# A re-ordered opening in an eight-core decoder layer

## The chip, the cores and the metric

The kernel runs on all 8 NeuronCores of one Trainium2 chip as one program, each core with an eighth of the tokens. The metric is device time in microseconds (us) of the slowest core. A core has TensorE (PE in the profile), VectorE (DVE), ScalarE (ACT), GpSimd (POOL) and SyncE (SP); cores 0 to 3 and 4 to 7 lie on two dies.

In some executions the cores of one die run at a lower granted clock, and the time is some per cent longer whatever the kernel. Such runs are called slow here, and are never set against fast ones. In two of the three batches of experiments (e1 to e4, e5 to e8, e9 to e12) one die was slow in many or all runs. There I compare the *undisturbed die*: of every run in which all four clocks of a die were above 0.99, the mean span of its four cores, averaged over the runs, with its standard error. Even there the mean clock lies between 0.996 and 1.000, and 0.001 of it is 1.2 us. So I also give some means *at equal clock*: each core's span times the granted clock on record for it, an estimate of the span had the clock never fallen. A difference that is gone at equal clock is one of the clock and not of the waits.

## The reference, cut to what matters

```python
h = rms_norm(x, g)
z = h @ w_in                    # columns: q 1024 | k 256 | v 256 | GLU value 1024 | GLU gate 1024
a = attn_prompt(q, k, v)        # window 128, q and k normed and rotated; 32 sample tokens use a cache
c = silu(layer_norm(causal_dwconv(u_val * sigmoid(u_gate))))   # width 31
x = x + concat([a, c]) @ w_out
x = x + relu(rms_norm(x) @ w_up) ** 2 @ w_down                 # hidden 8192
```

x is float32, 8192 prompt tokens and 32 sample tokens of 2048 features. A core multiplies 1032 to 1160 columns (tokens) at a time.

## The kernel before

The program records every operation of every engine in program order. A list scheduler then simulates time with fixed costs and emits, for each engine, the order in which its simulation could start the operations. Each engine executes that order strictly. One constant of this simulation is the DMA rate:

```python
    LAT = {"pe": 200, "act": 110, "dve": 110, "pool": 150}
    DMA_NS = 2000
    DMA_RATE = 290.0
    # ... cut ...
                if u[0].is_dma:
                    st = max(end, dma_free)
                    dma_free = st + u[0].nbytes / self.DMA_RATE
                    fin = dma_free + self.DMA_NS
```

The opening loads x in 16 chunks of 128 features, scales each to bf16 (`HT`), and multiplies it at once with the key and value weights. The query weights come after x:

```python
    for kc in range(16):
        xs_ = XST[kc % 8]
        xd.append(dma("sp", xs_(), R(xt_d[kc]), ..., after=[xd[kc - 6]] if kc >= 6 else []))
        dma("pool", WKV(kc), R(wkv_d[kc]), ..., after=[xd[max(kc - 4, 0)]] if kc >= 2 else [])
        ts("dve", HT(kc), xs_(), G1(kc), ALU.mult)
        # ... sums of squares cut ...
        for i in range(2):
            for h in range(2):
                mm(kps[i](h), WKV(kc, (128 * h, 128 * h + 128)), HT(kc, KPC[i]), kc == 0, kc == 15)
        for ti in range(8):
            v_mm(ti, vps[ti], kc, ...)
```

The output projection makes 16 blocks, each of 24 matmuls into three neighbouring PSUM banks, which VectorE then adds to x. Even blocks use banks 0 to 2; odd blocks 3 to 5 at first, later 4 to 6. Between them stand the last convolution and the statistics of the LayerNorm, which use banks 6 and 7:

```python
    def wo_half(dc, half, src, b0):
        accb = Buf("ps", psum[:, b0:b0 + 3, :], b0 * 2048, (3, 512), 4)
        # ... 24 matmuls into accb ...
        tt("dve", x3(), accb((0, 3), (0, PW)), x3(), ALU.add)

    def ln_stats():
        for pi, (a, b) in enumerate(PM):
            pm, pv = ps_f32(6, 1, (PW,)), ps_f32(7, 1, (PW,))      # banks 6 and 7
            # ... cut ...

    def wo_first(i):
        wo_half(DCO[i], 0, AT, 0 if i % 2 == 0 else 3 if i < 7 else 4)
        # ... cut ...

    for i in range(3):
        wo_first(i)
    conv_job(7, 0)
    # ... cut ...
    for i in range(3, 5):
        wo_first(i)
    ln_stats()
    for i in range(5, 16):
        wo_first(i)
```

## Time and profile before

| | before |
|---|---|
| median of three runs | 1233.95 us |
| spans of the cores in the profiled run | 1224.8 to 1233.1 us |
| TensorE busy, slowest core | 1195.2 us, 97% |
| idle of TensorE, mean of 8 cores: to 60 us / 60 to 150 / 150 to 320 / 320 to the MLP | 20.7 / 1.2 / 0.0 / 7.9 us |
| MLP: start, length, waits of TensorE (means) | 437.6, 791.0, 2.4 us |

The idle times are the length of a stretch less the busy time of TensorE in it, from the table by stretches, on every core; the MLP is taken to start with the run of matmuls that begins with the form 128x258 float32.

The table by stretches (the first column after the stretch is its length, then TensorE's busy time and, in brackets, its matmuls; the last columns are granted clock, DMA share, GB/s):

```profile
356.00:359.00 3.00, 3.00 (x12) 1.55 (x11) 3.00 (x3) 1.25 (x1) 0.00 (x0) 0.50 0.80 141
363.00:366.00 3.00, 3.00 (x23) 2.05 (x21) 3.00 (x3) 2.29 (x2) 0.00 (x0) 1.00 0.98 154
```

For about 3 us after the waits TensorE ran at half its clock: 12 matmuls in 3 us instead of 23. The cost is 12.30 - 72 x 0.149 = 1.6 us that no wait shows. Cores 0, 3, 4 and 5 have it (0.83 for the mean clock from 350 to 360 us). Cores 1, 2, 6 and 7 have the same waits of 1.55 and 2.06 us, keep a clock of 1.00, and do the same 72 matmuls in 10.62 us. What differs is how the waits fall into windows of 3.41 us. In the trace the stretches at half clock here last 3.41 us, and each follows 3.41 us in which TensorE did little.

### The profile page before, as it was taken

The numbers are of one execution on the slowest core, as the hardware profiler recorded it, in microseconds if no ns is written. First come the engines' busy times: TensorE is split into PE (matmuls) and PEld (weight loads), VectorE is DVE, ScalarE is ACT, GpSimd is POOL, SyncE is SP. The second block draws the span as 40 slices with busy tenths as digits, with TensorE's granted clock in tenths as the row PEclk, the third lists the DMA queues.
The fourth block names the chain that finished last, engine by engine and source line by source line (L and its number), as shares of the span: only waits on it lengthen the run. The fifth ranks groups of instructions, "written<-read, shape, count | busy, mean of one in ns | idle before, by whom it ended". The sixth has DMA issues, their size and how long they took to land.

```text
span 1233.1 us, 26343 instructions; the slowest of 8 cores (1224.8 to 1233.1 us)
## 1 busy us (share of the span) xinstructions
PE 1195.2 (97%) x10395; PEld 947.5 (77%) x10395; DVE 824.7 (67%) x1287; ACT 387.3 (31%) x538; POOL 77.8 (6%) x135
## 2 busy tenths in 40 slices
PE   5799999999989999999999999999999999999998
PEld 2466555555658888888888888888888888888887
DVE  5766756666386967676567667666767656766765
ACT  3464556654134634320004340002332001333000
POOL 2301000000001000000000000000000000000000
PEclk9999999999999999999999999999999999999999
DMA  9995265567839795539955455985454996454795
GB/s 235 218 161 68 46 114 96 104 149 150 217 70 198 197 229 99 106 81 244 232 112 103 86 103 147 245 193 99 74 114 94 229 241 119 79 94 79 183 244 193
DMA packets 55333, 180.27 MB, mean 146 GB/s; under 512 B 18836, under 2 KB 22036, under 8 KB 41236
## 3 DMA queue, kind: packets, MB, share of 16 engines
q0 software_dynamic: 29664, 90.74, 45.9%
q1 hardware_dynamic: 20508, 57.20, 13.9%
q10 hardware_dynamic: 5040, 30.65, 7.4%
q8 instruction: 84, 1.38, 0.4%
q14 instruction: 37, 0.30, 0.1%
HBM read 227.44 MB, written 34.68 MB: 213 GB/s over the span
## 4 chain that ended last, share of the span: by engine, by line
PE 87%; DMA 8%; DVE 2%; ACT 1%; issue 1%; SPq 0%; DVEq 0%; ACTq 0%; POOLq 0%
PE psum L623 87%; DMA arena<-xt 3%; DVE arena L587 2%; DMA arena<-x 2%; DMA x<-arena 1%; ACT arena L583 1%; DMA arena<-wkv 1%; DMA arena<-wup 1%; SPq L570 0%; DVEq L381 0%; ACT arena L605 0%; ACTq L381 0%; POOLq L381 0%; SPq L381 0%; DVE psum L615 0%
## 5 line engine op out<-in xcount | busy, mean ns | idle before, releaser
L623 PE MATMUL psum<-arena 128*128 128x258 f16 (+12 forms) x10395 | 1195.2, 287 | 34.1 <-DMA arena<-wkv 10.3
L623 PEld LDWEIGHTS psum<-arena 128*128 128x128 bf16 (+4 forms) x10395 | 947.5, 98 | 281.4 <-issue 80.6
L587 DVE TENSOR_TENSOR arena<-arena 128x1024 f16<-128x1024 bf16 (+11 forms) x751 | 504.8, 701 | 171.4 <-ACT arena L583 107.5
L587 DVE TENSOR_TENSOR arena<-psum,arena 128x516 f32<-128x516 f32 (+9 forms) x477 | 329.9, 699 | 211.8 <-PE psum L623 184.0
L583 ACT ACTIVATE arena<-arena 128x352 f32<-128x352 f32 (+11 forms) x264 | 250.3, 960 | 262.8 <-DVE arena L587 230.7
L605 ACT COPY arena<-psum 128x516 f32<-128x516 f32 (+2 forms) x68 | 39.1, 575 | 365.1 <-PE psum L623 341.4
L583 ACT ACTIVATE arena<-psum 128x512 bf16<-128x512 f32 (+9 forms) x142 | 77.9, 573 | 125.2 <-PE psum L623 124.6
L583 ACT ACTIVATE arena<-psum,arena 128x344 f32<-128x344 f32 (+6 forms) x54 | 30.5, 581 | 69.6 <-PE psum L623 69.4
L570 POOL DMA_DIRECT2D arena<-wdn x32 | 16.9, 528 | 382.1 <-PE psum L623 370.2
L570 POOL DMA_DIRECT2D arena<-wup x32 | 17.0, 531 | 375.8 <-PE psum L623 371.7
L600 DVE TENSOR_SCALAR arena<-arena 128x1160 bf16<-128x1160 f32 (+2 forms) x27 | 16.0, 592 | 14.0 <-DMA arena<-xt 12.9
L570 POOL DMA_DIRECT2D arena<-wo x16 | 11.2, 703 | 134.3 <-PE psum L623 134.3
L570 POOL DMA_DIRECT2D arena<-wu x16 | 8.5, 531 | 145.3 <-PE psum L623 142.4
L570 POOL DMA_DIRECT2D arena<-wkv x16 | 9.9, 620 | 27.8 <-DMA arena<-xt 26.9
L570 POOL DMA_DIRECT2D arena<-wq x16 | 8.5, 583 | 14.9 <-DMA arena<-xt 12.7
L583 ACT ACT_TABLE_LOAD x3 | 3.8, 1283 | 10.5 <-DMA arena<-xt 8.7
L600 DVE TENSOR_SCALAR arena<-psum 128x388 bf16<-128x388 f32 (+1 forms) x3 | 1.7, 561 | 5.8 <-PE psum L623 4.3
L570 POOL DMA_DIRECT2D arena<-cv x1 | 4.6, 4576 | 0.0
L607 DVE COPY arena<-arena 128x4 f32<-128x4 f32 (+1 forms) x11 | 3.4, 314 | 0.4
L611 DVE TENSOR_REDUCE arena<-arena 128x4 f32<-128x124 f32 x8 | 2.2, 280 | 0.5
L570 POOL DMA_DIRECT2D arena<-ckt x1 | 0.9, 892 | 14.1 <-DMA arena<-wu 14.1
L605 ACT CAST arena<-arena 128x128 bf16<-128x128 f32 (+2 forms) x6 | 1.5, 301 | 0.7 <-DMA arena<-cse 0.7
(10 smaller groups left out, 2.3 us busy)
## 6 DMA issues: line engine op xcount, KB each, us to landing
arena<-wup POOLq DMA_DIRECT2D x32, 1024.0 KB, 8.8
arena<-wdn POOLq DMA_DIRECT2D x32, 1024.0 KB, 12.0
arena<-x ACTq DMA_DIRECT2D x23, 1032.0 KB, 14.3
x<-arena SPq DMA_DIRECT2D x15, 1032.0 KB, 15.0
arena<-xt SPq DMA_DIRECT2D x16, 580.0 KB, 15.8
arena<-arena SPq DMA_DIRECT2D x128, 65.8 KB, 4.4
x<-arena SPq DMA_DIRECT2D x16, 516.0 KB, 10.4
arena<-wu POOLq DMA_DIRECT2D x16, 512.0 KB, 6.9
```

Of the source, the lines that this page charges most:

```text
L570: return P.add(eng, lambda e: e.dma_start(out=out.ap, in_=in_.ap), reads=[in_], writes=[out], key=key, group=group, final=final, after=aft ...
L583: return P.add("act", lambda e: e.activation(out=out.ap, in_=in_.ap, func=func, bias=b, scale=s), reads=rd, writes=[out], cost=cost("act", ...
L587: return P.add(eng, lambda e: e.tensor_tensor(out=out.ap, in0=in0.ap, in1=in1.ap, op=op), reads=[in0, in1], writes=[out], cost=cost(eng, o ...
L600: return P.add(eng, lambda e: e.tensor_scalar(out=out.ap, in0=in0.ap, scalar1=a, scalar2=b, op0=op0, **kw), reads=rd, writes=[out], cost=c ...
L605: return P.add("act", lambda e: e.copy(out=out.ap, in_=in_.ap), reads=[in_], writes=[out], cost=cost("act", out, [in_]))
L607: return P.add(eng, lambda e: e.tensor_copy(out=out.ap, in_=in_.ap), reads=[in_], writes=[out], cost=cost(eng, out, [in_]))
L611: return P.add("dve", lambda e: e.tensor_reduce(out=out.ap, in_=in_.ap, axis=AX.X, op=ALU.add), reads=[in_], writes=[out], cost=(size(in_) ...
L623: return P.add("pe", lambda e: e.matmul(out.ap, lhsT.ap, rhs.ap, start=start, stop=stop, skip_group_check=free), reads=[lhsT, rhs], writes ...
```

## The change

The intent is to give TensorE more work per byte of x in the opening. Chunks 0 to 7 of x feed keys and values; the partial sums are copied out of PSUM; query parts 0 and 1 are multiplied with the same chunks; chunks 8 to 15 feed queries only; the second half of keys and values comes last. x and the key/value weights come in transfers of two or four chunks. The other query parts alternate with the first GLU channel, attention is spread over fewer steps, and several small loads move. The output projection gets another bank and two operations move by one block. The scheduler's DMA rate goes from 290 to 315.

The core of the diff; "@@ cut" marks what is left out:

```diff
-    DMA_RATE = 290.0
+    DMA_RATE = 315.0
@@ cut
-    xt_d = din("xt", [16, 128, HW])
+    xt_d = din("xt", [8, 128, 2 * HW])
-    wkv_d = din("wkv", [16, 128, 512])
+    wkv_d = din("wkv", [128, 8192])
@@ cut
+    for k0, k1 in ((0, 1), (1, 2), (2, 4), (4, 6), (6, 8)):
+        x_in(k0, k1, [xd[0 if k0 == 4 else 1]] if k0 >= 4 else [])
+        wkv_in(k0, k1, [xd[1] if k0 == 4 else xd[3]] if k0 > 2 else [])
+    for kc in range(KH):                      # KH = 8
+        x_use(kc)
@@ cut: the K and V matmuls of this chunk
+    wq_in(0, 0, 4, [xd[5]])
+    wq_in(0, 4, 8, [xd[5]])
+    wq_in(1, 0, 8, [xd[5]])
+    for i in range(2):
+        cp("act" if i == 0 else "dve", KPART[i](), kps[i]())
@@ cut
+    for kc in range(KH, 16):
+        x_use(kc)
+        for p in range(2):
+            P.group()
+            for it in (2 * p, 2 * p + 1):
+                q_mm(it, kc)
+    wkv_in(8, 12, [xd[13]])
+    wkv_in(12, 16, [xd[13]])
@@ cut: 64 matmuls of 8 columns for the sample tokens' queries
+    for p in range(2):
+        for h in range(2):
+            for kc in range(16):
+                mm(qsb(2 * p + h), WQ(p, kc, (128 * h, 128 * h + 128)), HT(kc, (MC0 + 1024, MC0 + NM)), kc == 0, kc == 15)
@@ cut: in the loop over GLU channels
+        if c == 1:
+            gate_s = [P.streams["pool"][-1]]
+            dma("pool", KTS((0, SPC), (0, 2), (0, 127)), R(ckt), "cks", group=True, after=gate_s)
+            dma("pool", CVB(p=(0, 127)), R(cv[:, 1:128, :].rearrange("s k d -> k s d")), "cks", group=True, after=gate_s)
@@ cut
-        wo_half(DCO[i], 0, AT, 0 if i % 2 == 0 else 3 if i < 7 else 4)
+        wo_half(DCO[i], 0, AT, 0 if i % 2 == 0 else 3 if i < 15 else 4)
-    for i in range(3):
+    for i in range(4):
         wo_first(i)
     conv_job(7, 0)
@@ cut
-    for i in range(3, 5):
+    for i in range(4, 6):
         wo_first(i)
     ln_stats()
-    for i in range(5, 16):
+    for i in range(6, 16):
```

## The prediction

> **What bounds the kernel now.** I read the cores first (1224.8 to 1233.1 us, granted clock 0.995 to 1.000: an undisturbed run), then the page, then a table by stretches, the matmul timeline and the DMA queues of the opening.
>
> ```profile
> PE 1195.2 (97%) x10395; PEld 947.5 (77%) x10395; DVE 824.7 (67%) x1287; ACT 387.3 (31%) x538; POOL 77.8 (6%) x135
> PE   5799999999989999999999999999999999999998
> DMA  9995265567839795539955455985454996454795
> ```
>
> TensorE is busy in all but the first two of forty slices and one near slice 11. All idle time of TensorE is about 38 us; no change of order can win more than that, and the diff touches only what comes before the MLP. Stretches (us, then busy us per engine, clock, DMA share, GB/s written):
>
> ```profile
> 10.00:20.00 10.00, 7.21 (x28) 3.49 (x27) 7.04 (x7) 5.81 (x5) 3.16 (x6) 0.90 1.02 279
> 30.00:40.00 10.00, 7.66 (x51) 4.47 (x50) 8.25 (x8) 4.56 (x4) 2.95 (x4) 1.00 1.04 266
> 60.00:70.00 10.00, 10.00 (x74) 6.35 (x74) 2.45 (x4) 7.74 (x18) 1.71 (x4) 0.88 1.07 177
> ```
>
> Until about 54 us the DMA engines are full and TensorE is not; from there on it is the reverse. The matmul timeline shows how it waits:
>
> ```profile
> 9.66 6.07 PE L623 MATMUL psum<-arena 128*128 128x512 bf16 x24 [9.66 <-DVE arena L600]
> 18.52 6.81 PE L623 MATMUL psum<-arena 128*128 128x512 bf16 x36 [2.79 <-DMA arena<-wkv]
> ...
> 49.35 1.90 PE L623 MATMUL psum<-arena 128*128 128x512 bf16 x12 [0.77 <-DMA arena<-wkv]
> 51.77 1.90 PE L623 MATMUL psum<-arena 128*128 128x512 bf16 x12 [0.53 <-DMA arena<-wkv]
> 54.49 7.88 PE L623 MATMUL psum<-arena 128*128 128x256 bf16 x49 [0.82 <-ACT arena L605]
> ```
>
> Each of the 16 chunks of x feeds 12 matmuls (4 of 512, 8 of 256 columns), which then wait for the next chunk's weights. After 54.49 nothing waits until 129.13.
>
> Two sizes. Matmul rate, from a dense piece of the chain (matmuls of 256 and 258 columns, 257 on average): 77.00/690 = 111.6 ns, or 0.434 ns per column. So a chunk (4096 columns) is 1.78 us of work; its 1.90 holds one drain. Sixteen are 28.5 us, but the dense part starts at 54.5: **26.0 us are lost in the opening.** DMA rate, from the queues between 12 and 41 us (packets, MB written, share of 16 engines):
>
> ```profile
> 440.21 77.00 PE psum L623 x690
> q1 hardware_dynamic: 1703, 6.52, 70.3%
> q0 software_dynamic: 1547, 1.41, 33.3%
> ```
>
> x arrives as float32; the weights are cast on the way, so their 1.41 MB are 2.82 MB read. (6.52+2.82)/29 us = 322 GB/s in read bytes. All sizes below are read bytes.
>
> **What the Trainium skill says.** "DMA: Bandwidth & Descriptors", Bandwidth, gives 341 GB/s for a 1 MB transfer and advises batches of at least 1 MiB. This trace agrees in direction: the small wkv transfers took 33.3% of 29 us for 2.82 MB (292 GB/s), x with 0.59 MB each 320, and the 2 MB MLP slabs between 620 and 700 us 13.56 MB in 48.2% of 80 us, 351. Its section "Issuing engines are not separate DMA queues" says that all queues run on the same 16 engines; here the two shares add to 104%, so weights loaded earlier delay x. "TensorE: Matmul & The Clock Gate", Part 1, says that matmuls run at half rate until some 3.4 us of work, and again after an idle window; the first 24 took 6.07 us instead of 3.8. "VectorE: DVE Perf Modes", the perf-mode tier table, gives float32 tensor_tensor no fast mode; 128x1024 took 1222 ns here, about one element per cycle.
>
> **The change part by part.** The intent is to give TensorE more work per byte of x. Now K and V are all that x feeds while it loads. In the change, chunks 0 to 7 feed K and V, whose partial sums are copied out of PSUM; then half the weights of query parts 0 and 1 arrive and those are multiplied with the same chunks; chunks 8 to 15 feed only queries 0 and 1; the second half of K and V comes after x. x and wkv move in transfers twice or four times larger.
>
> Bytes: a chunk of x is 0.594 MB, its wkv 0.262, half a query part 1.049. The start of flow is about 3.3 us before as after; I take 325 GB/s, slightly above 322 for the larger transfers.
>
> Step 1, K|V on eight chunks: 8 x 0.856 = 6.85 MB, landed at 3.3+21.1 = 24.4 us. Chunks 6 and 7 land together: 0.82 us of DVE scaling and two chunks of 1.78 bring TensorE to 28.8. It needs PSUM banks back: half a microsecond for a 1.0 us copy that partly overlaps. 29.4.
>
> Step 2, queries 0 and 1 on chunks 0 to 7: 64 matmuls of 512 columns, 0.2222 us each, 14.2 us, to 43.6. Their 2.1 MB land by 3.3+8.95/0.325 = 30.9, in time.
>
> Step 3, the same on chunks 8 to 15: 14.2 us, to 57.8 if nothing waits. x is complete after 15.8 MB, at 51.9 us, or up to 55 because the next wkv is let in after chunk 13. From 54: 0.82 plus two chunks of 1.78 gives 58.4. Both limits agree: **58.4**.
>
> Step 4, the turn: the next matmul needs the bank of a query accumulator, which ACT must read (two of 0.70 us, a square of 1.03). Part of that lies beside the last matmuls; estimate 1.3 us lost. Dense from 59.7.
>
> Work done by then is 28.5/2 + 28.4 = 42.7 us, so 17.0 us are lost instead of 26.0. **Gain 9.0 us.**
>
> Added work: queries 0 and 1 now cover 1024 columns in blocks of 512, so the eight remaining columns need 64 more matmuls of 8 columns with full weights. 35 matmuls of 132 columns took 2.3 us here, 66 ns each; I put these at 55, so 3.5 us; 512 fewer columns give 0.2 back. **Cost 3.3 us.**
>
> Moved work: the six remaining query blocks alternate with the first GLU channel's six jobs, and attention is spread over 40 of 42 later jobs instead of over 48. TensorE's columns do not change. But the rotary work of DVE cannot start before cos and sin land, some 62 us, and EB is ready at about 66. From there: four query and two K blocks of 512 at 5.05 us (2.44+1.38+1.23), eight partial-sum additions at 0.69, six blocks of 344 at 3.64 (three of 873 ns, two of 513), small ones 4, GLU 6: 30.3+5.5+21.8+10 = 67.6, to 134. TensorE in the same stretch has about 78 us from 59.7: to 138. DVE is at 94%, and it executes in order, so some waits appear: **cost 1.5 us**, an estimate with nothing firmer behind it. The 1.2 us of waits that before has between 128 and 136 I count as staying in another form.
>
> The output projection starts one block later before the last convolution and keeps banks 3 to 5 longer; before waits some 7 us there on DVE (largest 2.1). I expect within 1 us.
>
> Sum: -9.0+3.3+1.5 = -4.2, and about half a microsecond for cleaner DMA: 1234.0-4.7 = **1229.3 us**.
>
> **The rivals.** First, DMA order decides instead: the query weights (2.1 MB for the second halves) sit before the last x; if they win more than half of the engines, or gates between transfers leave gaps, x completes at 58 to 60 and the net gain falls to 1 us or turns into a small loss: 1233 to 1236. For it: shares at 104%, full queues. Against: at least two large x transfers are always under way. Second, DVE becomes the bound between 66 and 140 us: if its 94% turn into 5 us of waits, 1233. For it: no slack, one shared set of RA and RBB buffers. Against: lateness can run into the attention stage, where DVE was at 62 to 69%. Third, larger descriptors take x well beyond 322, to the 351 of the slabs: first half landed at 22.8, TensorE alone then sets step 3, 1.6 us more: 1227 or 1228. Fourth, the 8-column matmuls cost only a short issue interval (25 ns): 2 us better.
>
> **Range and chances.** The rivals give 1227 to 1236; with the third and fourth together and milder DVE waits 1223. Range 1222 to 1236. 2% is 24.7 us: the whole loss of the opening is 26.0, of which about 10 precede the first byte, so faster by 2% has 0.01. Slower by 2% would need a stall of 25 us that nothing hints at: 0.02. Within 2%: 0.97.
>
> **What would show each step right or wrong.** Matmuls on chunks 0 to 7 end near 29 us; dense 512-column matmuls from there to 43; the last query matmul near 58; a gap of 1 to 2 us after it. 64 matmuls of 8 columns, total near 3.5 us. DVE above 90% from 66 to 134 us, few waits of TensorE on it. The first GLU channel done near 139 us. From 450 us on, the same trace shifted. I am wrong if x completes after 57, if TensorE waits more than 4 us in total between 60 and 140, or if attention (DVE denser) shows waits where before has none from 137 to 328.

## More of the kernel before

The MLP, from some 440 us to the end, multiplies in the manner of Strassen: for every 2 x 2 blocks it forms seven products. Weights arrive in slabs of four blocks; VectorE forms three or four sums of a slab's blocks (`left_sum`, its order chosen by the scheduler), and also takes the products out of PSUM:

```python
            elif n == 1:
                tt("dve", two(u2()), psv(1), two(ET()), ALU.add)     # out of PSUM
            # ... cut ...
            if slabs and 2 <= n < 6:
                left_sum(slabs[0], n - 2)                            # waits for the slab's DMA
```

Core 5, then core 1, each first the 3.41 us with the waits, then the 3.41 us after:

```profile
352.57:355.99 3.42, 1.35 (x11) 0.75 (x9) 3.42 (x4) 1.25 (x1) 0.70 (x1) 1.00 0.81 144
355.99:359.40 3.41, 3.41 (x14) 1.78 (x13) 3.36 (x3) 1.25 (x1) 0.00 (x0) 0.50 0.77 136
```

```profile
351.70:355.11 3.41, 1.39 (x10) 0.99 (x11) 3.41 (x4) 1.49 (x2) 0.70 (x1) 1.00 0.64 112
355.11:358.53 3.42, 3.42 (x26) 2.28 (x25) 3.42 (x4) 1.00 (x1) 0.45 (x1) 1.00 0.92 156
```

The four cores that fell were busy for 0.39 to 0.40 of that window, the four that did not for 0.41 to 0.59. Over all profiles (76 cores, from 30 us on), all 108 windows at full clock that were busy for less than 0.40 were followed by half clock, 6 of 46 between 0.40 and 0.50, and none of 1399 between 0.50 and 0.95. (So were 26 windows that count as busier than 0.95. Each of them holds 19 or 20 float32 matmuls of one column, some 2 of the 3.41 us; why such work does not keep the clock up is open.)

The prediction shows the lines of the opening. The later place where TensorE waits, the output projection, it mentions in one sentence only. This is the matmul timeline there, of the kernel before on core 5 (start, duration, then the run of matmuls, and in brackets the idle time before it and what ended that):

```profile
329.90 4.80 PE L623 MATMUL psum<-arena 128*128 128x344 bf16 x28 [0.50 <-DVE arena L587]
335.22 4.80 PE L623 MATMUL psum<-arena 128*128 128x344 bf16 x28 [0.51 <-DVE arena L587]
340.53 7.13 PE L623 MATMUL psum<-arena 128*128 128x344 bf16 x48 [0.51 <-DVE arena L587]
349.22 3.65 PE L623 MATMUL psum<-arena 128*128 128x344 bf16 x24 [1.55 <-DVE arena L587]
354.93 12.30 PE L623 MATMUL psum<-arena 128*128 128x344 bf16 x72 [2.06 <-DVE arena L587]
368.79 67.16 PE L623 MATMUL psum<-arena 128*128 128x344 bf16 x596 [1.55 <-DVE psum L615]
```

Runs of 24 matmuls are one output block. Five waits for VectorE and one for its memset make 6.7 us. The reader is to notice one thing more: 48 matmuls take 7.13 us, 149 ns each, but the 72 after the two longest waits take 12.30 us, 171 ns each.

## The result

| | median | range | runs |
|---|---|---|---|
| before, same chip | 1233.83 us | 1231.86 to 1255.63 | 14 |
| changed | 1233.26 us | 1227.82 to 1386.07 | 12 |

Ratios in this document are the mean time of one kernel's fast runs over that of the other's fast runs of the same rounds, so not quite the ratio of the medians. Here it is 0.9986, 95% interval 0.9968 to 1.0004: the same. Two of the changed kernel's runs (1386 and 1379 us) were slow ones and do not count. The fast runs scatter from 1227.8 to 1236.8 us; the profiled one took 1236.8.

The profile page of the changed kernel, core 7 (busy us; then TensorE's busy tenths in 40 slices):

```profile
PE 1197.0 (97%) x10395; PEld 943.9 (76%) x10395; DVE 835.4 (68%) x1300; ACT 384.3 (31%) x535; POOL 68.4 (6%) x118
PE   5999999999999999999999999899999999999998
```

Of before, the second slice stood at 7 and the twelfth at 8 (31 to 62 us and 339 to 370 us). Both are 9 now. In exchange the 26th (772 to 803 us, in the MLP) fell to 8. The opening's matmul timeline on this core:

```profile
19.42 5.31 PE L623 MATMUL psum<-arena 128*128 128x512 bf16 x24 [2.88 <-DMA arena<-wkv]
25.48 35.19 PE L623 MATMUL psum<-arena 128*128 128x512 bf16 x176 [0.75 <-DMA arena<-wkv]
62.00 1.76 PE L623 MATMUL psum<-arena 128*128 128x388 f32 x10 [1.32 <-DVE arena L587]
64.80 43.60 PE L623 MATMUL psum<-arena 128*128 128x256 bf16 x363 [1.04 <-DMA arena<-wkv]
```

From 25.48 us on TensorE is dense to 60.67: 48 matmuls finish chunks 4 to 7, then come the 128 of the queries. That is the shape that the change was made for. But the MLP waits more. First before (core 5), then changed (core 7), from 450 to 1200 us; the columns are who waited for whom, us in total, times, longest:

```profile
PE psum L623 <- DVE arena L587: 3.3, 6, 1.5
DVE arena L587 <- DMA arena<-wdn: 26.9, 15, 4.3
```

```profile
PE psum L623 <- DVE arena L587: 7.1, 12, 2.5
PE psum L623 <- ACT arena L605: 2.5, 1, 2.5
DVE arena L587 <- DMA arena<-wdn: 37.4, 20, 4.3
```

VectorE waits longer for weight slabs (`wdn`), and TensorE longer for VectorE. TensorE's one long wait on ScalarE ends at 779 us; the timeline of ScalarE (ACTq is its queue of DMA issues) shows its cause:

```profile
760.18 18.12 ACTq L570 DMA_DIRECT2D arena<-x  x2
778.51 0.59 ACT L605 COPY arena<-psum 128x516 f32<-128x516 f32 x1 [19.27 <-DMA x<-arena]
```

ScalarE has two loads of x to issue, of which one must wait for a store of x. It stands there for 18 us, and the copy out of PSUM, next in its order, is late.

By stages, means over the eight cores of each profiled run (the last two rows are experiments that follow, e5 and e9; the last one is over its four undisturbed cores):

| kernel | idle to 60 us | 60 to 150 | 150 to 320 | 320 to MLP | MLP starts | MLP length | waits in MLP |
|---|---|---|---|---|---|---|---|
| before | 20.7 | 1.2 | 0.0 | 7.9 | 437.6 | 791.0 | 2.4 |
| changed, first chip | 15.0 | 3.5 | 0.8 | 2.9 | 429.2 | 796.4 | 6.5 |
| changed, again on another chip | 14.6 | 3.2 | 0.6 | 2.6 | 427.8 | 791.3 | 2.8 |
| before with the output-projection part alone | 21.3 | 1.2 | 0.0 | 2.6 | 430.0 | 790.2 | 1.8 |

So the changed kernel reached the MLP 8.4 us earlier and on this chip gave 5.4 us of it back inside the MLP, in which the diff changes no instruction. Part of the 5.4 is this one run: it was the slowest of the ten fast ones, with a mean core of 1225.6 us where the 22 undisturbed dies of the changed kernel's runs on this chip have 1222.9 ± 0.5. Of the 7.6 us of idle time gained before the MLP, 5.0 come from the output projection and only 2.7 net from everything before it.

### The profile page after: what moved, and what is told of

It is laid out like the page before. It is cut to its first block, busy times and chain, and to the rows that moved or that the text cites. A ratio compares the mean times of both kernels' runs of the same rounds, so it can differ in the third digit from the quotient of the medians.

```text
span 1235.3 us, 26303 instructions; the slowest of 8 cores (1215.6 to 1235.3 us)
## 1 busy us (share of the span) xinstructions
PE 1197.0 (97%) x10395; PEld 943.9 (76%) x10395; DVE 835.4 (68%) x1300; ACT 384.3 (31%) x535; POOL 68.4 (6%) x118
## 4 chain that ended last, share of the span: by engine, by line
PE 82%; DMA 11%; DVE 3%; issue 2%; ACT 1%; SPq 1%; POOL 0%; DVEq 0%; ACTq 0%; POOLq 0%
PE psum L623 82%; DMA arena<-xt 3%; DVE arena L587 3%; DMA x<-arena 3%; ACT arena L583 1%; DMA arena<-x 1%; DMA arena<-wup 1%; DMA arena<-wkv 1%; DMA arena<-arena 1%; SPq L953 1%; DMA arena<-wq 1%; POOL arena L570 0%; ACT arena L605 0%; DVEq L381 0%; SPq L570 0%
## 5 line engine op out<-in xcount | busy, mean ns | idle before, releaser
L623 PE MATMUL psum<-arena 128*128 128x258 f16 (+10 forms) x10395 | 1197.0, 288 | 34.8 <-DMA arena<-wkv 15.7
L587 DVE TENSOR_TENSOR arena<-psum,arena 128x516 f32<-128x516 f32 (+7 forms) x485 | 336.7, 699 | 187.2 <-PE psum L623 175.7
L583 ACT ACTIVATE arena<-arena 128x512 f32<-128x512 f32 (+10 forms) x274 | 254.4, 950 | 276.7 <-DVE arena L587 229.1
L583 ACT ACTIVATE arena<-psum 128x512 bf16<-128x512 f32 (+9 forms) x140 | 74.7, 567 | 134.5 <-PE psum L623 134.1
L583 ACT ACTIVATE arena<-psum,arena 128x512 f32<-128x512 f32 (+7 forms) x42 | 23.1, 575 | 48.9 <-PE psum L623 48.3
L570 POOL DMA_DIRECT2D arena<-wkv x7 | 4.4, 632 | 35.1 <-DMA arena<-xt 34.2
L570 POOL DMA_DIRECT2D arena<-wq x8 | 4.5, 566 | 30.2 <-DMA arena<-wkv 14.8
L600 DVE TENSOR_SCALAR arena<-psum,arena 128x512 f32<-128x512 f32 x4 | 2.8, 744 | 0.0
```

What stands on the lines that cost most here:

```text
L570: return P.add(eng, lambda e: e.dma_start(out=out.ap, in_=in_.ap), reads=[in_], writes=[out], key=key, group=group, final=final, after=aft ...
L583: return P.add("act", lambda e: e.activation(out=out.ap, in_=in_.ap, func=func, bias=b, scale=s), reads=rd, writes=[out], cost=cost("act", ...
L587: return P.add(eng, lambda e: e.tensor_tensor(out=out.ap, in0=in0.ap, in1=in1.ap, op=op), reads=[in0, in1], writes=[out], cost=cost(eng, o ...
L600: return P.add(eng, lambda e: e.tensor_scalar(out=out.ap, in0=in0.ap, scalar1=a, scalar2=b, op0=op0, **kw), reads=rd, writes=[out], cost=c ...
L623: return P.add("pe", lambda e: e.matmul(out.ap, lhsT.ap, rhs.ap, start=start, stop=stop, skip_group_check=free), reads=[lhsT, rhs], writes ...
```

## The experiments

Theory 1: the constant DMA_RATE re-ordered VectorE and ScalarE in the MLP, and that order costs what was given back. The built orders show that it can: in the MLP, 157 positions on VectorE and 8 on ScalarE differ between the changed kernel at 315 and at 290, and none on TensorE, GpSimd or SyncE; at 290 the MLP's order is that of before, and before at 315 gets the changed kernel's. An excerpt for ScalarE, 315 (-) against 290 (+), once in each quarter of the MLP:

```
 L605 TensorCopy arena<-psum 128x516 x3
-L570 DMACopy arena<-x 128x2064
-L605 TensorCopy arena<-psum 128x516
-L570 DMACopy arena<-x 128x2064
-L605 TensorCopy arena<-psum 128x516
+L570 DMACopy arena<-x 128x2064 x2
+L605 TensorCopy arena<-psum 128x516 x2
```

On VectorE the order of 315 places sums of slabs ahead of reads of PSUM that stood in front of them at 290: a scheduler that believes in faster transfers expects slabs sooner.

Theory 2, the rival: the MLP begins 8 us earlier against the same weight transfers, on all cores, and contends with them whatever the order. Theory 3, for the front: the gain lies in the new bank and not in the opening.

### e1 to e4: the constant, and each engine's order

On one chip, five rounds. e1 is the changed kernel with the old constant, e2 the reverse:

```diff
 e1 (changed)                    e2 (before)
-    DMA_RATE = 315.0            -    DMA_RATE = 290.0
+    DMA_RATE = 290.0            +    DMA_RATE = 315.0
```

e1 also gets back old orders in the opening (48 positions on TensorE). So e3 and e4 keep 315 everywhere but in the MLP of one engine, whose order is spliced in from a second scheduling:

```diff
-    P.schedule()
+    late_order, P.streams = order_at(290.0), order_at(315.0)
+    for e in ('act',):                      # e3; ('dve',) in e4
+        a, b = P.streams[e], late_order[e]
+        cut = min(i for i in range(len(a)) if a[i].idx >= mlp)
+        while set(a[:cut]) != set(b[:cut]):
+            cut += 1
+        P.streams[e] = a[:cut] + b[cut:]
```

> The changed kernel with the scheduler's assumed DMA rate put back from 315 to 290; nothing else. It restores the MLP's order on DVE and ACT exactly as before has it, and moves a few instructions in the opening. Theory 1 (the constant re-ordered the MLP and gives the gain back there): 1225 to 1228 us, faster than before by some 6 to 9 us, MLP from its first norm matmul to the end about 791 us on the mean core as before, not 796. Theory 2 (cores that arrive earlier collide in HBM, whatever the order): MLP still about 796 us, time 1231 to 1235.

> The kernel before with the assumed DMA rate put up from 290 to 315; nothing else: PE, POOL and SP keep their order, DVE and ACT get exactly the MLP order of the changed kernel. Theory 1: slower than before by the 5 us of the mean core or the 8 to 10 of the slowest: 1238 to 1243 us, the MLP about 796 us on the mean core. Theory 2: 1234 us, the MLP at 791.

> The changed kernel, with only ACT's order in the MLP taken from the schedule at 290 (8 positions differ: in each quarter one PSUM copy stands ahead of an x load again, instead of behind it). Theory 1a (ACT's copy held behind a load that waits for a store): most of the 5 us of the mean core come back, 1227 to 1230. Theory 1b (DVE's slab sums too early in the queue): no change, 1231 to 1235.

> The changed kernel, with only DVE's order in the MLP taken from the schedule at 290 (157 positions differ: the sums that wait for a weight slab stand later again). Theory 1b (slab sums too early): 1226 to 1230, MLP about 791 to 792 us on the mean core. Theory 1a: no change, 1231 to 1235.

Measured; before had a median of 1245.85 us on this chip, and many runs were slow, so the ratios say little:

| | median | ratio to before | undisturbed die | MLP waits, mean / worst core |
|---|---|---|---|---|
| before | 1245.85 | | 1229.2 ± 0.4 | |
| e1, changed at 290 | 1239.63 | 0.9945 (0.9913 to 0.9978) | 1220.5 ± 0.8 | 1.6 / 2.3 |
| e2, before at 315 | 1254.51 | 1.0058 (0.9964 to 1.0153) | 1229.3 ± 0.6 | 3.0 / 9.2 |
| e3, ScalarE at 290 | 1238.01 | 0.996 (0.9871 to 1.0049) | 1222.0 ± 0.6 | 3.1 / 4.9 |
| e4, VectorE at 290 | 1242.14 | 0.9971 (0.9905 to 1.0038) | 1220.7 ± 0.6 | 2.1 / 4.5 |

The waits point where theory 1 does: least with both engines at 290, more with either at 315, and 9.2 us on one core of before at 315. The spans as they stand do not confirm it: before at 315 is as fast as before on the undisturbed die. But the granted clock cost before 4.4 us there and e2 only 2.6. At equal clock e2 is 1.8 ± 0.5 us slower than before, and e1, e4 and e3 are 8.8, 7.6 and 6.4 us faster (± 0.5): the ranking that theory 1 foretold, at 1 to 2.4 us instead of the expected 5 and more. No engine's order can be blamed alone.

### e5 and e6: the changed kernel again, and with the MLP of 290

Another chip, undisturbed in most runs, five rounds. e5 is the changed kernel without an edit. e6 splices both engines:

```diff
-    for e in ('act',):
+    for e in ('act', 'dve'):
```

> The changed kernel itself once more, on the chip of the next three runs, since the last chip granted some cores a lower clock and no profile of the changed kernel was taken there. What is compared is TensorE's waits in the MLP (norm matmul to end), mean of the 8 cores: 6.5 us in its first profile, 2.4 in the one of before. Theory 1 (order): again 5 to 8 us. If it is below 3.5, the first profile was an accident and there is nothing to explain by the order.

> The changed kernel, its opening untouched, ACT and DVE in the MLP in the order of the schedule at 290. Theory 1 (order): TensorE's waits in the MLP 1.5 to 2.5 us on the mean core, 4 to 5 us below the changed kernel on the same chip, and the time 4 to 8 us below it. Theory 2 (early arrival makes cores collide): 5 to 8 us of waits as in the changed kernel.

| | median | ratio to before | undisturbed dies, 0 and 1 |
|---|---|---|---|
| before | 1232.62 | | 1227.3 ± 0.2, 1227.5 ± 0.2 |
| e5 | 1227.51 | 0.9953 (0.9941 to 0.9965) | 1219.7 ± 0.6, 1219.3 ± 0.6 |
| e6 | 1224.41 | 0.9936 (0.9923 to 0.9949) | 1218.8 ± 0.5, 1218.1 ± 0.3 |

On this chip the unedited change is 0.5% faster than before, where the first chip had shown nothing. Part of this is the metric: the cores of the changed kernel spread more, and on the first chip the slowest one hid what the mean core gained (1222.9 us against 1228.6 in before's one profile). e5 also failed the test that it was made for: its MLP waits are 2.8 us in the mean, not 5 to 8, and lie below the 3.5 under which the expectation would have had nothing left to explain by the order. So the first profile's 6.5 us is not what this order usually costs, and what is left to explain is small. e6 is 2.1 us below e5 in the mean of the fast runs (1224.4 of four against 1226.5 of five, standard error of the difference 0.7); the two ratios' intervals still overlap. Waits in the MLP of e6, core 1, from 450 to 1200 us:

```profile
PE psum L623 <- DVE arena L587: 1.3, 5, 0.6
DVE arena L587 <- DMA arena<-wdn: 17.1, 11, 3.4
```

In the mean of the eight cores, VectorE waits 18.3 us for these slabs (before 24.2, the changed kernel 45.0 on the first chip and 41.0 in e5), and TensorE waits 2.1 us in the MLP (2.4, 6.5 and 2.8). So VectorE's waits follow the order on both chips, but in e5 little of them reached TensorE. The expectation of e6, 4 to 5 us fewer waits and 4 to 8 us of time, missed in size: 0.7 and 2.1 us. e6 is faster than both kernels.

### e7 and e8: the order much earlier and much later

If order is the cause, a rate that promises slabs much earlier must be worse, and one that promises them much later should not wait for slabs at all. If early arrival is the cause, both must be about as good as e6.

```diff
-    late_order, P.streams = order_at(290.0), order_at(315.0)
+    late_order, P.streams = order_at(400.0), order_at(315.0)     # e7; 230.0 in e8
```

> The same, with the MLP's order from a schedule that believes in 400 bytes per ns: 373 DVE and 40 ACT positions differ from 290, against 157 and 8 at 315. Theory 1: waits in the MLP grow beyond those of the changed kernel, above 8 us on the mean core. Theory 2: no dependence on the assumed rate, as in the changed kernel.

> The same, with the MLP's order from a schedule that believes in 230 bytes per ns: slab sums later still (358 DVE and 14 ACT positions differ from 290). Theory 1: waits no higher than at 290, 1 to 2.5 us; perhaps the best of the four. Theory 2: as in the changed kernel, 5 to 8 us.

e7 took 1280.49 us (ratio 1.0383, 1.0356 to 1.041), e8 1276.72 (1.0357, 1.0345 to 1.037). e7, same stretch:

```profile
PE psum L623 <- DVE arena L587: 30.6, 16, 4.4
DVE arena L587 <- DMA arena<-wdn: 65.0, 21, 6.2
```

and e8:

```profile
PE psum L623 <- DVE arena L587: 23.6, 8, 7.7
DVE arena L587 <- DMA arena<-wdn: 21.2, 6, 6.1
```

In both the MLP starts where e6's does (429.5 and 429.0 against 428.2 us) and is 48 to 49 us longer. With the order of 400, VectorE stands in front of slabs that have not come while products wait in PSUM behind it. With 230 it seldom waits for a slab, but the sums come late and TensorE waits for them, more seldom and longer. TensorE's waits in the MLP are 36.8 us in the mean in e7 and 40 in e8. e7's expectation (above 8) came true; e8's (1 to 2.5, "perhaps the best of the four") was wrong, for a later order costs as much as an earlier one. So the MLP's length hangs on this order, on both sides of 290, with no change to a single instruction. That rules out theory 2 as the main cause: an equally early start was good with one order and bad with two others. Over all profiles, undisturbed dies alone, waits of TensorE in the MLP were at most 4.0 us on 36 cores with the order of 290 (seven kernels, means 1.8 to 2.4) and up to 11.9 us on 20 cores with that of 315 (three kernels, means 2.8, 4.4 and 6.5).

### e9: the output-projection part alone

The kernel before with only the output-projection part of the diff:

```diff
-        wo_half(DCO[i], 0, AT, 0 if i % 2 == 0 else 3 if i < 7 else 4)
+        wo_half(DCO[i], 0, AT, 0 if i % 2 == 0 else 3 if i < 15 else 4)
-    for i in range(3):
+    for i in range(4):
@@ and range(4, 6), range(6, 16) as in the change
```

> The kernel before with the output-projection part of the change alone (later switch from PSUM bank 3 to bank 4, one block more before the last convolution); the orders of VectorE, ScalarE and TensorE in the MLP are those of before. If the 5 us that the changed kernel saved between 320 us and the MLP come from this part: TensorE idle from 320 us to the MLP falls from 7.9 to 2.3-3.0 us (mean of cores), the MLP starts 5 us earlier with its length unchanged, and the time is 4 to 5 us below before. If instead they come from the opening (attention spread over fewer steps, loads moved): idle stays at 7-8 us and the time within 1 us of before.

This and the next three ran in a batch in which die 0 was slow in every run (clock near 0.95), so the times are those of slow runs: before 1279.95 us, e9 1275.24. The undisturbed die tells: before 1228.0 ± 0.5 us, e9 1219.9 ± 0.2, which is 8.1 us less. The projection in e9, core 4:

```profile
318.82 44.59 PE L623 MATMUL psum<-arena 128*32 128x512 bf16 x328
364.91 53.75 PE L623 MATMUL psum<-arena 128*128 128x256 bf16 x484 [1.50 <-ACT arena L583]
```

Of the six waits of before one of 1.5 us is left, on another engine, and the clock stays at 1.00 there. Idle from 320 us to the MLP fell to 2.6 us as expected, but the MLP starts 7.8 us earlier, not 5 (430.0 against 437.8 us in the mean of cores 4 to 7 of the profiles). Waits account for 5.2 us, the half clock in the projection for 0.85 (1.7 us on cores 4 and 5 each, none on 6 and 7). Most of the rest is not the projection's: these four cores lost some 2.4 us to half clock elsewhere before the MLP in before's profile, most of it in the opening, and 0.4 in e9, whose idle time to 60 us was 0.6 us longer. The same holds for the 8.1 us: the granted clock cost before 3.35 us over the whole span and e9 0.84. At equal clock e9 is 5.6 ± 0.4 us faster, which is what its waits account for; the other 2.5 ± 0.9 us are clock, and only part of that is due to the projection.

The built order shows what the edit did. VectorE adds the 16 output blocks to x in this order (blocks numbered as the program issues them):

```
before:           0 1 2 3 4 5 6 8 10 7 9 12 11 14 13 15
bank 3 to i < 15: 0 1 2 3 4 5 6 7 8 9 10 11 12 13 14 15
```

From block 7 on, before put odd blocks into banks 4 to 6, and bank 6 is also that of the statistics. The scheduler could not start block 7 until the statistics were read, and took the even blocks 8 and 10 first. Blocks 6, 8 and 10 all use banks 0 to 2, so each must wait until VectorE has read the one before it, and 7 and 9 do the same in banks 4 to 6. With banks 3 to 5 odd and even blocks alternate, and VectorE reads one while TensorE fills the other. A build with the bank edit alone, without the moved convolution and statistics, has the same order 0 to 15, and one with the moved operations alone keeps the order of before; neither was run.

### e10: the larger transfers alone

The kernel before, with x and the key/value weights in the new layouts and two chunks to a transfer after the first two, and nothing else:

```diff
-        xd.append(dma("sp", xs_(), R(xt_d[kc]), ...))
-        dma("pool", WKV(kc), R(wkv_d[kc]), ...)
+        if kc < 2 or kc % 2 == 0:
+            n = 1 if kc < 2 else 2
+            xd += [dma("sp", t(), R(xt_d[kc // 2][:, HW * (kc % 2):HW * (kc % 2) + HW * n]), ...)] * n
+            dma("pool", ..., R(wkv_d[:, 512 * kc:512 * (kc + n)]), ...)
```

> The kernel before with nothing of the change but the larger transfers of x and of the key/value weights (two chunks each). If the opening gained from the re-ordering: idle of TensorE before 60 us stays at 19 to 22 us (before 20.7) and the time within 1.5 us of before. If it gained from larger transfers: idle falls to 15-17 us, the time by 4 to 6 us.

Undisturbed die 1229.3 ± 0.4 us against before's 1228.0 ± 0.5; idle before 60 us 21.1 against 20.7. In the old order larger transfers gain nothing by themselves; what the opening gained, it gained by the re-ordering (with the larger transfers; the re-ordering was not run without them). The last dense stretch even begins later, at 54.2 to 56.8 us on the eight cores against 52.8 to 54.5 in before.

### e11: the load of the cached values in two pieces

In e6 four cores have a new wait near 200 us, 1.3 to 3.4 us long, on a GLU weight. On core 4 the weight was issued at 171.00 us, just behind the cached values (`cv`, 127 partitions, issued at 166.43). The issues of e6, core 4, from 90 to 330 us (size of one, median time from issue to landing):

```profile
arena<-ckt POOLq DMA_DIRECT2D x1, 254.0 KB, 5.8
arena<-cv POOLq DMA_DIRECT2D x1, 254.0 KB, 35.6
```

Two loads of the same size, one after the other: 5.8 and 35.6 us. In before the same load took 28.4 us, but nothing stood behind it. "DMA: Bandwidth & Descriptors", section "Why a DMA increments its semaphore by 16 and not by 1", says that an outer dimension of 127 divides by no engine count but 1, so one engine carries everything. The trace agrees: on core 4 of e6 the load's 508 packets of 512 bytes go one after another from 171.7 to 201.6 us, at most 3 at a time. e11 is e6 with that load split:

```diff
-            dma("pool", CVB(p=(0, 127)), R(cv[:, 1:128, :]...), "cks", group=True, after=gate_s)
+            dma("pool", CVB(p=(0, 112)), R(cv[:, 1:113, :]...), "cks", group=True, after=gate_s)
+            dma("pool", Ref(CVB(p=(112, 127)).ap, ()), R(cv[:, 113:128, :]...), "cks", group=True, after=gate_s)
```

(The second piece is left out of the program's dependency tracking by hand, because that tracks byte ranges over all partitions and would let the second wait for the first for ever; it goes out behind the first in the same queue. A first build without this was found to deadlock and was not run.)

> The changed kernel with the old order in the MLP (as in the run with late units ordered at 290) and the load of the cached values (127 partitions) in two pieces, of 112 and of 15 partitions. If the new wait for a GLU weight near 200 us comes from this load being slow in front of it in the queue: the load lands in under 10 us instead of 35, the waits of TensorE from 150 to 320 us go from about 1.2 us in the mean (3.4 on the worst core) to below 0.4, and the time falls by 1 to 2 us against that run. If the wait comes from the bus: no change.

The issues of e11 on core 4:

```profile
arena<-cv POOLq DMA_DIRECT2D x1, 224.0 KB, 8.2
...
arena<-cv POOLq DMA_DIRECT2D x1, 30.0 KB, 9.4
```

In e11 the same 508 packets take 5.0 us, up to 21 at a time. No core of e11 or of the next run waits for a GLU weight, so the cause of that wait is settled. The rest of the expectation missed: idle from 150 to 320 us is 0.7 us in the mean, not below 0.4, because three cores wait 1.2 to 2.4 us near 318 us for a copy from SBUF to SBUF, a wait that the changed kernel also had on the first chip and that I had not counted. The undisturbed die took 1218.6 ± 0.6 us: 9.3 below before, where e6 was 9.0 below its own before. The expected 1 to 2 us are not there.

### e12: other gates in the opening

e11, with the weights of chunks 4 and 5 let go earlier and x of chunks 6 and 7 later:

```diff
-        x_in(k0, k1, [xd[0 if k0 == 4 else 1]] if k0 >= 4 else [])
-        wkv_in(k0, k1, [xd[1] if k0 == 4 else xd[3]] if k0 > 2 else [])
+        x_in(k0, k1, [xd[0 if k0 == 4 else 3]] if k0 >= 4 else [])
+        wkv_in(k0, k1, [xd[0] if k0 == 4 else xd[3]] if k0 > 2 else [])
```

> The same, and in the opening the third transfer of key/value weights is let go two chunks earlier and the last transfer of the first half of x two chunks later. If the first step ended late because those weights came behind x: TensorE's work on the fifth chunk starts at 22-23 us instead of 25.5, idle before 60 us falls from 14.5 to 12-13 us, the time by 1 to 2.5 us more: 8.5 to 12 us below before. If the bytes alone set the first step: idle stays at 14-15 us, as then the sixth to eighth chunks wait instead.

On four cores TensorE went on without a wait from the third chunk (19.2 to 20.3 us). Yet the fifth began at 24.2 to 25.6 us there, no earlier than on the same cores of e11 (24.1 to 25.1) and not at the expected 22 to 23: on all four the clock from 20 to 24 us was only 0.50 to 0.73, so what the wait gave up, the slow clock took. Idle before 60 us was 14.2 us in the mean (14.3 in e11), not 12 to 13, and the queries ended at 60.3 to 62.4 us. The expectation missed, and neither of its theories had the clock. Undisturbed die 1218.2 ± 0.3 us, 9.8 below before; from e11 it can't be told apart (0.5 ± 0.7).

## Why the prediction was right or wrong

The total was right: 1229.3 us predicted, 1233.26 measured on the first chip and 1227.51 on the second, both in the range and within 2%. The sum behind it was wrong in its parts. Step by step:

**Step 1, keys and values on eight chunks: too early by 3.2 us.** Predicted end 29.4 us; measured 25.48 for the start of the fifth chunk plus four chunks of 1.78, 32.6. VectorE could start to scale the last two chunks only at 27.54 us. From 3 to 12 us the queues of the changed kernel moved (packets, MB written, share)

```profile
q1 hardware_dynamic: 341, 1.69, 72.6%
q0 software_dynamic: 272, 0.26, 27.4%
```

that is 1.69 + 2 x 0.26 = 2.21 MB read in 9 us, 246 GB/s, and 320 GB/s only from 12 to 28 us. Before has the same start (2.23 MB), so it was there to be read. ("Some 10 us before the first byte", in its range, is a slip as well: bytes flow from 3.3 us on, and 9.66 is the first matmul.) That start costs (322 - 246) x 9 / 322, about 2.1 us. TensorE had a share too: chunks 3 and 4 took 5.31 us instead of 3.56, at a low clock after the waits for the first ones. So the step had two bounds close together, and I had summed one of them, with a rate too high at its start.

**Steps 2 and 3, the queries: right in rate, late by what step 1 was late.** The 128 matmuls ran from 32.64 to 60.67 us, 219 ns each where the prediction had 222. They ended at 60.7 us against 58.4, and x was not what they waited for: the first rival did not come true.

**Step 4, the turn: right.** 1.32 us against 1.3. A wait of 0.6 to 1.4 us for the second half of the key/value weights, on six of eight cores, was not in the sum.

**The gain of 9.0 us** therefore came out as 5.7 to 6.1 us less idle time before 60 us, of which 2.0 to 2.3 us were given back before 150 us.

**The cost of 3.3 us for small matmuls was too high.** All 70 matmuls of 8 columns (six of them the rotary norms) took 2.2 us, 31 ns each, so the 64 took 2.0 us and not 3.5. The fourth rival was right, nearly to its 25 ns. The row, from the groups by shape between 60 and 150 us:

```profile
L623 PE MATMUL psum<-arena 128*128 128x8 bf16 x70 | 2.2, 166 | 0.0
```

(The 166 ns in it is one matmul from its start to its modelled end; the busy time is the 2.2 us.)

**VectorE did not become the bound.** Predicted 94% busy from 66 to 134 us, measured 56.48 of 68 us, 83%. TensorE waited for it only at the turn. In total it waited 2.5 to 3.9 us between 60 and 140 us, just inside the 4 us that the prediction had named as a sign against it.

**Attention: waits where before has none**, as the prediction named among the signs against it: 0.6 to 1.2 us in the mean, from the weight queued behind the cached values (shown by e11) and from the SBUF copies (not explained further).

**The output projection: this step failed.** The prediction said "I expect within 1 us". The part was worth 8.1 ± 0.6 us by itself (e9), 5.6 of them at equal clock; the whole change was worth 7.9 us on the second chip by the first measure, 8.1 by the other. I had counted instructions that moved and looked at which banks were kept longer, but not at which blocks could start while another was read. I also had the half clock before me and did not see it. "TensorE: Matmul & The Clock Gate", Part 1, puts the fall to half rate after an idle window of some 3.4 us. Here the window was not idle: it fell on four cores that had worked for 0.39 to 0.40 of such a window, and not on the four that had worked for 0.41 to 0.59 of it. The measurement decides: waits of 1.55 and 2.06 us were enough where enough of them lay in one window.

**The MLP: this step failed too.** "From 450 us on, the same trace shifted" overlooked the first line of the diff, which changes no instruction but their order on two engines. On the first chip the MLP was 5.4 us longer. That the order of 315 leaves VectorE waiting for slabs is shown by the traces, and that this order can decide the length of the MLP is shown by e7 and e8 and, with a small difference, by e6. The price of 315 against 290 is 1 to 2.4 us: 2.1 in time from e5 to e6, 1.8 at equal clock from before to e2. Why the MLP of the first profile was 5.4 us longer is open: that run was the slowest of its kernel's fast ones, and the order of 290 was not run there, so that it would have avoided all of this is argued only.

Added up, at equal clock and with ± 0.4 to 0.6 on each: the projection gave 5.6 us. The whole change gave 8.1 us with the MLP at 315 (e5), so the opening with all else gave 2.5; with the MLP at 290 (e6, e11 and e12: 8.9, 9.0 and 9.1) it gave 3.3 to 3.5, where I had predicted 4.7. Without that correction the projection has 8.1, and the opening with all else between nothing (7.9 - 8.1) and 1.7; e11, of the same batch as e9, is 1.3 ± 0.6 below it. Either way the opening gave less than predicted and the projection much more than the "within 1 us". That the total fell so close was luck: the misses nearly cancelled, with the MLP's order taking a part.

## What to carry to other kernels

Before moving work, read every stretch in which the bounding engine waits, and ask of each wait which buffer it is for: one PSUM bank shared with a short side job undid the alternation of two accumulators. Mending it, in the part of the diff that e9 runs, was worth more than a re-written opening. (That the bank and not the moved operations restored the alternation is shown by the built orders, not by a run.) Where a scheduler orders the engines, compare the built orders over the whole program and not only where the diff is: a constant of its cost model is a change to every stage. And read the granted clock after each group of waits, because the slow matmuls behind them are booked as busy.

## What the Trainium skill lacked or had wrong

- "TensorE: Matmul & The Clock Gate", Part 1: its table has the half rate begin after an idle window of some 3.4 us. It gives no share of work below which a window counts as idle. Here the clock was 0.50 for 3.41 us after windows of 3.41 us in which TensorE was busy for 0.39 to 0.40 (cores 0, 3, 4 and 5), and stayed at 1.00 after 0.41 to 0.59 (cores 1, 2, 6 and 7). Over all profiles all 108 windows below 0.40 were followed by half clock, 6 of 46 between 0.40 and 0.50, and none of 1399 between 0.50 and 0.95.
- "DMA: Bandwidth & Descriptors", section "Why a DMA increments its semaphore by 16 and not by 1": as an exception measured on trn2 it has some copies of 127 partitions that GpSimd issues use all engines. The load of 127 partitions here took 35.6 us for 254 KB and became 8.2 and 9.4 us in pieces of 112 and 15 partitions, and its packets went one after another, which fits the page's rule (one engine) and not its exception.
- The same page, Bandwidth, has no figure for the start of a kernel: from 3 to 12 us the transfers moved 246 GB/s here, and 320 from 12 to 28 us.
